# A hybrid decoder block on one core: reordering its first thirty microseconds

## The chip, the cores and the metric

The kernel runs on one core of a Trainium2 chip. The metric is the device time of one execution in microseconds; lower is better. The core has five engines that run side by side and wait for one another through semaphores: TensorE (matrix products into PSUM), VectorE, ScalarE, GpSimd and SyncE, whose queue issues most transfers.

## The reference, cut to what matters

One layer of a decoder block on x of 256 tokens by 1024 channels, in float32. What the change touches is the beginning: a normalisation, one wide projection, and the first stages of the branches.

```python
def rms_norm(x, w):
    y = xf * lax.rsqrt(jnp.mean(xf * xf, axis=-1, keepdims=True) + EPS)
    return (y * w.astype(jnp.float32)).astype(x.dtype)

def token_mixer(h, w_in, ...):
    z = h @ w_in
    rq, rk, rv, rg, sb, sc, sx, nq, nkv, ng, mg = jnp.split(z, IN_OFFSETS, axis=-1)
    y_ret = retention(...)
    y_sc = sb * causal_dwconv(sc * sx, sc_conv_w)
    k_c, v_c, k_s, v_s, k_w, v_w = jnp.split(nkv..., 6, axis=2)
    y_nsa = nsa_attention(nq, k_c, v_c, k_s, v_s, k_w, v_w, jax.nn.sigmoid(ng), ...)
    g_ret, g_sc, g_nsa = jnp.split(jax.nn.sigmoid(mg), N_BRANCH, axis=-1)
    merged = g_ret * (y_ret @ w_ret_out) + g_sc * (y_sc @ w_sc_out) + g_nsa * (y_nsa @ w_nsa_out)
    return merged @ w_mix_out

h = rms_norm(x, attn_norm_w[l])
x = x + token_mixer(h, w_in[l], ...)
h = rms_norm(x, ffn_norm_w[l])
x = x + conv_glu_ffn(h, w_ffn_up[l], ffn_conv_w[l], w_ffn_down[l])
return rms_norm(x, final_norm_w)
```

## The kernel before

**Products in three parts.** Every float32 operand is split into a rounded high half and a low half (the remainder), and a product is made as high x high + high x low + low x high (`mm3`, through `mm`, line 167). A weight comes in pieces of 1 MB, as two halves of 128 x 1024; each half is loaded by SyncE into a raw buffer (`Item.load`, L134; four buffers, `RAWB`), cast to its high half on ScalarE (L142), and the low half is subtracted on VectorE (L143). The split halves live in a ring of five pairs, and while the room `m` is idle in a sixth (`w_m`).

**The stream.** `stream` walks a list of pieces: at each it issues the loads of the pieces up to `la` ahead, splits the next one, and emits the products of the present one (`consume`) and what was put off by `later`. The program is laid out by a scheduler that may reorder instructions that do not depend on one another; `keep_in_program_order` pins one.

**The front.** x comes transposed (`xT_s`: channels on partitions, eight K-chunks of 256 tokens), chunk 0 on ScalarE's queue, the others by `head_load` (L289). `head_chunk` makes the halves `xw` of x times the norm weight, without the row scale (high on ScalarE L293, low on VectorE L294; the tiles are named ynsah and ynsal). `vv` is five items that multiply x by the value weights and the attention gates' weights (560 columns, eight K-chunks of 280 KB). They run on `xw`, and the row scale is applied to the sums (`vv_evac`, L516 and L517). Meanwhile `head_square` squares x on ScalarE (L300) and adds the squares on GpSimd (L301, L303); between the products of K-chunks 6 and 7 `head_rest` sums over the channels with four tiny products and raises to the power -1/2 on GpSimd (`row_rstd`, L307 and L308), and `head_spread` copies the result along all partitions as `rstd`. `head_h` multiplies xT_s by rstd on GpSimd (L335) and makes the scaled halves `hT` (L337 on ScalarE, L338 on VectorE).

**The order of the pieces.** Behind `vv`: kc and vc (compressed keys and values, on `xw`, scaled in `cmp_raw_evac`, L371, whose result is then moved by a transfer, dd<-dd, that ScalarE's queue issues, L372), ks and kw (keys, on `hT`), two pieces of the first merge gate (512-column products, `t_pair`, `mg_evac` L772), a w1 piece (first layer of the compression), two more gate pieces, w1, two query pieces, and so on. The first nine items run with a look-ahead of two; behind them two wide raw buffers in the rooms of x and of the squares are added, and the look-ahead is four.

Before all this stand eight warm-up products of ones (`WARM`).

Of the kernel before, what the change touches and what calls it, by code (L numbers as in the profile page):

```python
# [18 lines left out]
S = 256  # L19
# [44 lines left out]
def kernel(  # L64
# [38 lines left out]


    RAWB, SPB = 4, 5
    WARM = 8

# [14 lines left out]

    raws, loads = [raw_ring, raw_ring], [0]

    class Item:
        def __init__(self, srcs, consume, pull=0, side=0):
            self.srcs, self.consume, self.pull, self.side = srcs, consume, pull, side
            self.raw, self.parts = [], []  # L130

        def load(self):
            for (ap, n), r in zip(self.srcs, raws[loads[0] % len(raws)](len(self.srcs))):
                nc.sync.dma_start(r[:, :n], ap)  # L134
                self.raw.append(r)
            loads[0] += 1

        def split(self):
            for (ap, n), r in zip(self.srcs, self.raw):
                hi, lo = splitters[count[0] % len(splitters)](self.side)  # L140
                count[0] += 1
                A.copy(hi[:, :n], r[:, :n])  # L142
                V.tensor_sub(lo[:, :n], r[:, :n], f32(hi[:, :n]))  # L143
                self.parts.append((hi, lo))

# [144 lines left out]

    def head_chunk(k0, k1):
        for k in range(k0, k1):
            A.activation(xw[0][:, k, :], xT_s[:, k, :], AF.Copy, scale=attw(k))  # L293
            V.scalar_tensor_tensor(  # L294
                xw[1][:, k, :], xT_s[:, k, :], attw(k), f32(xw[0][:, k, :]), op0=OP.mult, op1=OP.subtract
            )

    def head_square(c):
        cs = slice(2 * c, 2 * c + 2)
        A.activation(sq[:, cs, :], xT_s[:, cs, :], AF.Square)  # L300
        G.tensor_add(sq[:, 2 * c, :], sq[:, 2 * c, :], sq[:, 2 * c + 1, :])  # L301
        if c:
            G.tensor_add(sq[:, 0, :], sq[:, 0, :], sq[:, 2 * c, :])  # L303

    def row_rstd(ps, rs):

# [22 lines left out]
    def head_spread():  # L329
        spread(rs0, sq[:, 1, :], rstd)  # L330

    def head_h(half):
        for c in range(2 * half, 2 * half + 2):
            x2k = xT_s[:, 2 * c : 2 * c + 2, :]
            G.tensor_tensor(x2k, x2k, rstd.unsqueeze(1).to_broadcast([128, 2, S]), op=OP.mult)  # L335
            for k in (2 * c, 2 * c + 1):
                A.activation(hT[0][:, k, :], xT_s[:, k, :], AF.Copy, scale=attw(k))  # L337
                V.scalar_tensor_tensor(  # L338
                    hT[1][:, k, :], xT_s[:, k, :], attw(k), f32(hT[0][:, k, :]), op0=OP.mult, op1=OP.subtract
                )  # L340
# [1 line left out]

    att_es = ExitStack()
    at = att_es.enter_context(pool("at"))
    kd = [at.tile([128, 4, 528], F32R, name=n) for n in ("kdh", "kdl")]
    vz = at.tile([128, 2, 2, 4, 128], F32R, name="vz")
    vbd = at.tile([128, 4, 4, 128], F32R, name="vbd")
    sg = at.tile([128, 2, 48], F32, name="sg")
# [12 lines left out]
    splitters.append(w_m)  # L361
    blk = {}

    def cmp_raw_evac(kv):
        def evac(ps):
            p4 = ps.rearrange("p (b t) -> p b t", b=2)
            d = cp.tile([128, 4, S], F32, tag="dd", name="dd", bufs=2)
            dv = d.rearrange("p (b two) t -> p b two t", two=2)
            for par in range(2):
                r = slice(par * 64, par * 64 + 64)  # L370
                V.tensor_tensor(dv[0:64, :, par, :], p4[r], rstd[r].unsqueeze(1).to_broadcast([64, 2, S]), op=OP.mult)  # L371
            nc.scalar.dma_start(d[64:128, :, 0 : S - 1], d[0:64, :, 1:S])  # L372
            wait_pieces(4 if kv else 2, lambda: cmp_blocks(kv, d))

        return evac

# [15 lines left out]

    def key_evac(name):
        def evac(ps):
            p4 = ps.rearrange("p (b t) -> p b t", b=2)
            kv4 = [k.rearrange("p (b two) t -> p b two t", two=2) for k in kd]
            job = []
            for par in range(2):
                r = slice(par * 64, par * 64 + 64)
                for t in range(2):  # L400
                    c = KCOL[(name, t)]
                    job.append((p4[r, :, t * 128 : (t + 1) * 128], [k[r, :, par, c : c + 128] for k in kv4]))
            for src, dst in job:
                A.copy(dst[0], src)
            for src, dst in job:
                V.tensor_sub(dst[1], src, f32(dst[0]))
            for par in range(2):
                r = slice(par * 64, par * 64 + 64)
                o = slice(64 - par * 64, 128 - par * 64)
                c = min(KCOL[(name, t)] for t in range(2))  # L410
                for k in kv4:
                    nc.gpsimd.dma_start(k[o, :, par, c : c + 256], k[r, :, par, c : c + 256])

        return evac
# [104 lines left out]
    def vv_items():  # L519
        st = {}  # L520

        def go(ks, off):
            def run(parts):
                if ks[0] == 0:
                    st["a"] = [bank("aux"), bank("aux")]
                    st["w"] = bank("aux")
                for k in ks:
                    hi, lo = parts[k - off]
                    for t in range(2):
                        a = slice(t * 128, (t + 1) * 128)  # L530
                        l = (xw[0][:, k, a], xw[1][:, k, a])
                        mm3(st["a"][t][:, 0:304], l, (hi[:, 0:304], lo[:, 0:304]), k == 0, k == 7)
                        mm3(
                            st["w"][:, t * 256 : t * 256 + 256],
                            l,
                            (hi[:, 304:560], lo[:, 304:560]),
                            k == 0 and t == 0,
                            k == 7,
                        )
                        if (k, t) == (6, 0):  # L540
                            head_rest()
                        if (k, t) == (7, 0):
                            head_spread()
                if ks[-1] == 7:
                    for t in range(2):
                        vv_evac(t, 0, st["a"][t])
                        A.activation(sg[:, t, :], st["a"][t][:, 256:304], AF.Tanh, scale=rsh[:, t : t + 1])
                        V.tensor_scalar(sg[:, t, :], sg[:, t, :], 1.0, 0.5, op0=OP.add, op1=OP.mult)  # L548
                    for t in range(2):
                        vv_evac(t, 1, st["w"][:, t * 256 : t * 256 + 256])  # L550
                    cg = sg[:, 0, :].rearrange("p (h b) -> p h b", b=3)[:, :, 0:1]
                    V.tensor_scalar(cg, cg, cmt[:, CM_ANY : CM_ANY + 1], None, op0=OP.mult)

            return run

        res = []
        for ks in ([0], [1], [2, 3], [4, 5], [6, 7]):
            res.append(Item([(wv[:, j, :], 560) for j in ks], go(ks, ks[0])))
        return res


    ynsa = []
# [203 lines left out]

    thg = {}

    def mg_evac(n, c):
        def evac(t, ps):  # L770
            th = yp.tile([128, 512], F32, tag="thg", name="thg", bufs=4)
            A.activation(th, ps, AF.Tanh, scale=0.5)  # L772
            thg[n, c, t] = th

        return evac
# [30 lines left out]
    GATE = {"o_ret": 0, "o_sc": 1, "o_nsa": 2}  # L806
    YY = {}

    def gate(n, **kw):

        return [p for c in range(2) for p in t_pair("mg", GATE[n] * 4 + 2 * c, hT, mg_evac(n, c), **kw)]

    def proj(n, **kw):
        return [p for c in range(2) for p in t_pair(n, 2 * c, lambda: YY[n], o_evac(n, c), **kw)]

    vv = vv_items()
    g_sc = gate("o_sc")
    items = vv + [
        then(piece("kc", 0, f_consume(xw, cmp_raw_evac(0), enter=True), side=SIDE), lambda: head_h(0), before=True),
        then(piece("vc", 0, f_consume(xw, cmp_raw_evac(1)), side=SIDE), lambda: head_h(1), before=True),  # L820
        piece("ks", 0, f_consume(hT, key_evac("ks")), side=SIDE),
        piece("kw", 0, f_consume(hT, key_evac("kw")), side=SIDE),
        g_sc[0],
        g_sc[1],
        piece("w1", 0, w1_consume(0, 0)),
        g_sc[2],
        g_sc[3],
        piece("w1", 1, w1_consume(0, 1)),
        nqp(0),
        nqp(1),  # L830
# [2 lines left out]
        scx(1),  # L833
        piece("w1", 3, w1_consume(1, 1)),
    ]
    vv[0].load()
    head_load(1, 2)
    vv[1].load()
    head_load(2, 4)
    vv[2].load()  # L840
    head_load(4, 6)
    head_load(6, 8)
    head_chunk(0, 1)
    vv[0].split()
    head_chunk(1, 2)
    vv[1].split()
    head_chunk(2, 4)
    vv[2].split()
    vv[3].load()
    nc.sync.dma_start(cvt, cv)  # L850
    nc.sync.dma_start(cmt, cm)
    for c in range(4):
        if c > 1:
            head_chunk(2 * c, 2 * c + 2)
        head_square(c)
    V.tensor_scalar(rethalf, x_s[:, KB : 2 * KB], 0.5, None, op0=OP.mult)
    att = attention()
    late = []
    plan = "x4 b0 x2 x3 q2 x6 b1 x5 x7 b2 q3 b3 s0 s1 n0 n1 s2 s3 n2 n3".split()
# [3 lines left out]
        late.append(made[e[0]](int(e[1])))  # L863
        late[-1].pull = (36 * (n + 1)) // len(plan) - 36 * n // len(plan)

    cut = 9
    stream(items[:cut], nxt=items[cut:])

    def wide(tag):
# [499 lines left out]
```

## Time and profile before

| | |
|---|---|
| median of 3 runs | 610.75 us (610.47 to 611.11) |
| profiled execution: its time | 611.28 us |
| profiled execution: span from first to last instruction | 609.5 us |
| TensorE busy | 597.8 us, 98% of the span |
| VectorE, ScalarE, GpSimd busy | 477.2, 388.1 and 27.0 us |
| mean granted TensorE clock | 0.998 |
| moved by transfers | 111.82 MB, mean 183 GB/s |

The busy share is an average over stages. Products are pipelined and their ends are modelled, so the starts of successive products tell more than the busy share. A row of the timeline gives start and duration of one instruction or of several merged ones (x2, x3), then engine, line, operation, output and inputs, and in brackets the idle time of the engine before it and what ended it. PE is TensorE, DVE is VectorE, ACT is ScalarE, POOL is GpSimd, SPq is SyncE's queue.

### The profile page before, as it was taken

To read this page: it belongs to the slowest core of one execution; us is meant where nothing else is said; L and a number is where in the kernel's file an instruction comes from. 1 tells how busy PE (TensorE), PEld (TensorE's weight loads), DVE (VectorE), ACT (ScalarE), POOL (GpSimd) and SP (SyncE) were. 2 spreads that over 40 slices of the span, in tenths; PEclk is the share of its full clock that TensorE was granted. 3 is DMA by queue.
4 is the path that set the end of the run, shared out by engine and by line. 5 is a ranking of instruction groups with operands and counts; after the bars stand their busy time and mean duration, and the time that the engine had idled before them with its cause. 6 is when DMAs were issued, how large, how long until landed. Compare 5 with 4: busy or idle time off the path is not lost.

```text
span 609.5 us, 10654 instructions
## 1 busy us (share of the span) xinstructions
PE 597.8 (98%) x3967; PEld 543.4 (89%) x3967; DVE 477.2 (78%) x936; ACT 388.1 (64%) x758; POOL 27.0 (4%) x36
## 2 busy tenths in 40 slices
PE   8899999999999999999999999999999999999995
PEld 7898899999999888898888888888999999999995
DVE  5788877799999878688567977568798887777754
ACT  6548865788998888644444565447756555555533
POOL 4603000000000000000000100000000000000000
PEclk9999999999999999999999999999999999999999
DMA  7789937443434444466565487575437765666401
GB/s 257 242 273 278 359 127 228 156 136 123 155 104 140 138 140 137 145 207 206 195 196 159 126 269 242 191 267 173 131 117 266 222 205 195 208 208 194 153 1 69
DMA packets 33139, 111.82 MB, mean 183 GB/s; under 512 B 3648, under 2 KB 5952, under 8 KB 32960
## 3 DMA queue, kind: packets, MB, share of 16 engines
q1 hardware_dynamic: 30384, 106.07, 53.0%
q10 hardware_dynamic: 1552, 4.03, 2.1%
q0 software_dynamic: 1152, 1.05, 1.1%
q8 instruction: 31, 0.51, 0.4%
q14 instruction: 20, 0.16, 0.1%
HBM read 108.51 MB, written 1.05 MB: 180 GB/s over the span
## 4 chain that ended last, share of the span: by engine, by line
PE 89%; ACT 3%; DVE 3%; DMA 2%; issue 1%; SPq 0%; ACTq 0%; DVEq 0%
PE ps_mm L167 66%; PE ps_aux L167 20%; PE ps_aux L642 1%; DVE wlo L143 1%; DMA xT_s<-in_xT_dram 1%; DMA raw<-in_wp_dram 1%; ACT whi L142 1%; ACT P L619 1%; PE ps_mm L797 1%; ACT ph L645 0%; DVE sg L548 0%; DVE ynsal L294 0%; PE ps_aux L671 0%; PE ps_aux L991 0%; DVE pl L646 0%
## 5 line engine op out<-in xcount | busy, mean ns | idle before, releaser
L143 DVE TENSOR_TENSOR wlo<-raw,whi 128x1024 fp32r<-128x1024 f32 (+1 forms) x187 | 225.7, 1213 | 75.1 <-ACT whi L142 73.2
L142 ACT CAST whi<-raw 128x1024 fp32r<-128x1024 f32 (+1 forms) x187 | 192.1, 1034 | 120.1 <-PE ps_mm L167 75.5
L167 PE MATMUL ps_mm<-h,whi 128*128 128x256 f32 (+1 forms) x576 | 99.0, 277 | 0.0
L167 PE MATMUL ps_mm<-hTh,whi 128*128 128x256 f32 (+1 forms) x328 | 92.2, 281 | 0.0
L167 PE MATMUL ps_mm<-hTl,whi 128*128 128x256 f32 x328 | 91.6, 279 | 0.0
L167 PE MATMUL ps_mm<-hTh,wlo 128*128 128x256 f32 x328 | 91.5, 279 | 0.0
L167 PEld LDWEIGHTS ps_mm<-h,whi 128*128 128x128 f32 x576 | 87.5, 188 | 0.7
L167 PE MATMUL ps_mm<-h,wlo 128*128 128x256 f32 x288 | 79.7, 277 | 0.0
L167 PEld LDWEIGHTS ps_mm<-hTh,whi 128*128 128x128 f32 x328 | 61.9, 189 | 0.6 <-issue 0.4
L167 PEld LDWEIGHTS ps_mm<-hTl,whi 128*128 128x128 f32 x328 | 61.8, 188 | 0.4 <-DVE hTl L338 0.2
L167 PEld LDWEIGHTS ps_mm<-hTh,wlo 128*128 128x128 f32 x328 | 61.7, 188 | 0.4
L167 PE MATMUL ps_mm<-whi,hTh 128*128 128x512 f32 x152 | 59.9, 394 | 0.0
L167 PE MATMUL ps_mm<-wlo,hTh 128*128 128x512 f32 x152 | 59.5, 392 | 0.0
L167 PE MATMUL ps_mm<-whi,hTl 128*128 128x512 f32 x152 | 59.4, 391 | 0.0
L167 PEld LDWEIGHTS ps_mm<-h,wlo 128*128 128x128 f32 x288 | 54.1, 188 | 0.0
L619 ACT ACTIVATE P<-P,st 128x16 f32<-128x16 f32 (+2 forms) x96 | 38.1, 401 | 1.1 <-DVE st L614 0.5
L167 PE MATMUL ps_aux<-wlo,acth 128*128 128x512 f32 (+1 forms) x94 | 35.5, 377 | 0.0
L167 PE MATMUL ps_aux<-whi,acth 128*128 128x512 f32 (+1 forms) x94 | 35.4, 377 | 0.0
L167 PE MATMUL ps_aux<-whi,actl 128*128 128x512 f32 (+1 forms) x94 | 35.3, 376 | 0.0
L167 PEld LDWEIGHTS ps_mm<-wlo,hTh 128*128 128x128 f32 x152 | 28.6, 188 | 6.0 <-DVE wlo L143 0.5
L167 PEld LDWEIGHTS ps_mm<-whi,hTl 128*128 128x128 f32 x152 | 28.6, 188 | 5.8
L167 PEld LDWEIGHTS ps_mm<-whi,hTh 128*128 128x128 f32 x152 | 28.6, 188 | 5.6
(263 smaller groups left out, 1200.5 us busy)
## 6 DMA issues: line engine op xcount, KB each, us to landing
raw<-in_wp_dram SPq DMA_DIRECT2D x184, 512.0 KB, 4.4
raw_w<-in_wp_dram SPq DMA_DIRECT2D x10, 512.0 KB, 6.7
raw<-in_wv_dram SPq DMA_DIRECT2D x8, 280.0 KB, 4.8
x2b<-in_xt_dram ACTq DMA_DIRECT2D x1, 1024.0 KB, 4.8
xT_s<-in_xT_dram SPq DMA_DIRECT2D x3, 256.0 KB, 6.4
rct<-in_rc_dram ACTq DMA_DIRECT2D x1, 768.0 KB, 5.0
kdh<-kdh POOLq DMA_DIRECT2D x4, 128.0 KB, 8.4
kdl<-kdl POOLq DMA_DIRECT2D x4, 128.0 KB, 9.7
```

The costliest lines, as they stand in the source:

```text
L142: A.copy(hi[:, :n], r[:, :n])
L143: V.tensor_sub(lo[:, :n], r[:, :n], f32(hi[:, :n]))
L167: return T.matmul(o, l, r, start=start, stop=stop, skip_group_check=True)
L619: A.activation(pp, pp, AF.Exp, bias=st[:, r : r + 1], scale=-1.0, accum_out=sm[:, r : r + 1])
L642: T.transpose(pt[:, dst : dst + 128], u["P"][(t, pr)][:, c : c + 128], ident)
L797: T.transpose(pt[:, b * 128 : (b + 1) * 128], src[:, c * 512 + b * 128 : c * 512 + (b + 1) * 128], ident)
```

## The change

- Loads: the loads of the value pieces, of kc and of vc are all put on SyncE's queue before any split is emitted. The last two value items load into the rooms of the key halves (`kdh`, `kdl`), vc into that of the queries (`qs`). The two constant tables (cvt, cmt) are loaded behind them.
- Order: the casts and squares of the front are pinned to one order; the first value cast is on VectorE. The row statistic stands behind the last value product, the spread of rstd behind kc's products. vc is split before the value evacuation.
- The first merge gate (four pieces) runs right behind vc, on `xw` unscaled; the row scale is applied in its tanh (`mg_evac`, `rsh`). Before each of its pieces one quarter of `hT` is made. Then w1, ks, kw, w1. The look-ahead of four begins two items later.
- Engines: the multiplication by rstd and the additions of squares go from GpSimd to VectorE; the small steps on `sg` go from VectorE to ScalarE and behind vc.
- ten warm-up products in place of eight; a 288-column first product in vc and ks.

```diff
     RAWB, SPB = 4, 5
-    WARM = 8
+    WARM = 10
 
...
 
+    exact = [False]
+
+    def in_order(ins):
+        if exact[0]:
+            tc.keep_in_program_order(ins)
+
...
             self.srcs, self.consume, self.pull, self.side = srcs, consume, pull, side
+            self.room = None
             self.raw, self.parts = [], []
...
         def load(self):
-            for (ap, n), r in zip(self.srcs, raws[loads[0] % len(raws)](len(self.srcs))):
+            room = self.room or raws[loads[0] % len(raws)]
+            for (ap, n), r in zip(self.srcs, room(len(self.srcs))):
                 nc.sync.dma_start(r[:, :n], ap)
...
 
-        def split(self):
+        def split(self, cast=A.copy):
             for (ap, n), r in zip(self.srcs, self.raw):
...
                 count[0] += 1
-                A.copy(hi[:, :n], r[:, :n])
+                in_order(cast(hi[:, :n], r[:, :n]))
                 V.tensor_sub(lo[:, :n], r[:, :n], f32(hi[:, :n]))
...
         for k in range(k0, k1):
-            A.activation(xw[0][:, k, :], xT_s[:, k, :], AF.Copy, scale=attw(k))
+            in_order(A.activation(xw[0][:, k, :], xT_s[:, k, :], AF.Copy, scale=attw(k)))
             V.scalar_tensor_tensor(
...
         cs = slice(2 * c, 2 * c + 2)
-        A.activation(sq[:, cs, :], xT_s[:, cs, :], AF.Square)
-        G.tensor_add(sq[:, 2 * c, :], sq[:, 2 * c, :], sq[:, 2 * c + 1, :])
+        in_order(A.activation(sq[:, cs, :], xT_s[:, cs, :], AF.Square))
         if c:
-            G.tensor_add(sq[:, 0, :], sq[:, 0, :], sq[:, 2 * c, :])
+            V.tensor_add(sq[:, 0:2, :], sq[:, 0:2, :], sq[:, cs, :])
+        if c == 3:
+            V.tensor_add(sq[:, 0, :], sq[:, 0, :], sq[:, 1, :])
 
...
 
-    def head_h(half):
-        for c in range(2 * half, 2 * half + 2):
+    def head_h(c):
+        if True:
             x2k = xT_s[:, 2 * c : 2 * c + 2, :]
-            G.tensor_tensor(x2k, x2k, rstd.unsqueeze(1).to_broadcast([128, 2, S]), op=OP.mult)
+            V.tensor_tensor(x2k, x2k, rstd.unsqueeze(1).to_broadcast([128, 2, S]), op=OP.mult)
             for k in (2 * c, 2 * c + 1):
...
     at = att_es.enter_context(pool("at"))
-    kd = [at.tile([128, 4, 528], F32R, name=n) for n in ("kdh", "kdl")]
+    kd = []
+
+    def key_room(tag):
+
+        z = at.tile([128, 2, 1056], F32, tag=tag, name="raw_k")
+        return lambda n: [z[:, i, 0:1024] for i in range(n)]
+
+    def query_room(n):
+        return [at.tile([128, 1024], F32, tag="qs", name="raw_q", bufs=2) for _ in range(n)]
+
...
 
-    def cmp_raw_evac(kv):
+    def cmp_raw_evac(kv, first=None):
         def evac(ps):
+            if first:
+                first()
             p4 = ps.rearrange("p (b t) -> p b t", b=2)
...
             nc.scalar.dma_start(d[64:128, :, 0 : S - 1], d[0:64, :, 1:S])
-            wait_pieces(4 if kv else 2, lambda: cmp_blocks(kv, d))
+            wait_pieces(5 if kv else 3, lambda: cmp_blocks(kv, d))
 
...
         def evac(ps):
+            if not kd:
+                kd.extend(at.tile([128, 4, 528], F32R, tag=n, name=n) for n in ("kdh", "kdl"))
             p4 = ps.rearrange("p (b t) -> p b t", b=2)
...
                         )
-                        if (k, t) == (6, 0):
-                            head_rest()
-                        if (k, t) == (7, 0):
-                            head_spread()
                 if ks[-1] == 7:
+                    head_rest()
+                    items[6].split()
                     for t in range(2):
+                        A.activation(sg[:, t, :], st["a"][t][:, 256:304], AF.Tanh, scale=rsh[:, t : t + 1])
                         vv_evac(t, 0, st["a"][t])
-                        A.activation(sg[:, t, :], st["a"][t][:, 256:304], AF.Tanh, scale=rsh[:, t : t + 1])
-                        V.tensor_scalar(sg[:, t, :], sg[:, t, :], 1.0, 0.5, op0=OP.add, op1=OP.mult)
                     for t in range(2):
                         vv_evac(t, 1, st["w"][:, t * 256 : t * 256 + 256])
-                    cg = sg[:, 0, :].rearrange("p (h b) -> p h b", b=3)[:, :, 0:1]
-                    V.tensor_scalar(cg, cg, cmt[:, CM_ANY : CM_ANY + 1], None, op0=OP.mult)
 
...
+
+    def nsa_gates():
+        for t in range(2):
+            A.activation(sg[:, t, :], sg[:, t, :], AF.Copy, scale=0.5, bias=0.5)
+        cg = sg[:, 0, :].rearrange("p (h b) -> p h b", b=3)[:, :, 0:1]
+        A.activation(cg, cg, AF.Copy, scale=cmt[:, CM_ANY : CM_ANY + 1])
 
...
 
-    def mg_evac(n, c):
+    def mg_evac(n, c, early):
         def evac(t, ps):
             th = yp.tile([128, 512], F32, tag="thg", name="thg", bufs=4)
-            A.activation(th, ps, AF.Tanh, scale=0.5)
+            A.activation(th, ps, AF.Tanh, scale=rsh[:, t : t + 1] if early else 0.5)
             thg[n, c, t] = th
...
 
-    def gate(n, **kw):
-
-        return [p for c in range(2) for p in t_pair("mg", GATE[n] * 4 + 2 * c, hT, mg_evac(n, c), **kw)]
+    def gate(n, early=False, **kw):
+
+        act = xw if early else hT
+        return [p for c in range(2) for p in t_pair("mg", GATE[n] * 4 + 2 * c, act, mg_evac(n, c, early), **kw)]
 
...
     vv = vv_items()
-    g_sc = gate("o_sc")
+    g_sc = gate("o_sc", early=True)
     items = vv + [
-        then(piece("kc", 0, f_consume(xw, cmp_raw_evac(0), enter=True), side=SIDE), lambda: head_h(0), before=True),
-        then(piece("vc", 0, f_consume(xw, cmp_raw_evac(1)), side=SIDE), lambda: head_h(1), before=True),
-        piece("ks", 0, f_consume(hT, key_evac("ks")), side=SIDE),
+        piece("kc", 0, f_consume(xw, cmp_raw_evac(0, head_spread), enter=True), side=SIDE),
+        piece("vc", 0, f_consume(xw, cmp_raw_evac(1), enter=True), side=SIDE),
+        *[then(g_sc[c], lambda c=c: head_h(c), before=True) for c in range(4)],
+        piece("w1", 0, w1_consume(0, 0)),
+        piece("ks", 0, f_consume(hT, key_evac("ks"), enter=True), side=SIDE),
         piece("kw", 0, f_consume(hT, key_evac("kw")), side=SIDE),
-        g_sc[0],
-        g_sc[1],
-        piece("w1", 0, w1_consume(0, 0)),
-        g_sc[2],
-        g_sc[3],
         piece("w1", 1, w1_consume(0, 1)),
...
     ]
+    kc, vc = items[5:7]
+    vv[3].room, vv[4].room, vc.room = key_room("kdh"), key_room("kdl"), query_room
     vv[0].load()
...
     head_load(4, 6)
+    vv[3].load()
     head_load(6, 8)
+    vv[4].load()
+    kc.load()
+    vc.load()
+    nc.sync.dma_start(cmt, cm)
+    nc.sync.dma_start(cvt, cv)
+    exact[0] = True
     head_chunk(0, 1)
-    vv[0].split()
+    vv[0].split(V.tensor_copy)
     head_chunk(1, 2)
...
     vv[2].split()
-    vv[3].load()
-    nc.sync.dma_start(cvt, cv)
-    nc.sync.dma_start(cmt, cm)
-    for c in range(4):
-        if c > 1:
-            head_chunk(2 * c, 2 * c + 2)
-        head_square(c)
-    V.tensor_scalar(rethalf, x_s[:, KB : 2 * KB], 0.5, None, op0=OP.mult)
+    head_square(0)
+    head_chunk(4, 6)
+    vv[3].split()
+    head_square(1)
+    head_chunk(6, 8)
+    vv[4].split()
+    head_square(2)
+    head_square(3)
+    exact[0] = False
+    then(vc, lambda: V.tensor_scalar(rethalf, x_s[:, KB : 2 * KB], 0.5, None, op0=OP.mult))
+    then(vc, nsa_gates)
     att = attention()
...
 
-    cut = 9
+    cut = 11
     stream(items[:cut], nxt=items[cut:])
...
```

## Rows read from the trace of the kernel before

**Rows 1.** Waits of TensorE in the first 90 us: total, times, longest

```profile
PE ps_mm L167 <- DVE wlo L143: 1.7, 1, 1.7
```

**Rows 2.** All waits of TensorE from 90 us to the end

```profile
PE ps_aux L167 <- ACT ph L645: 0.4, 2, 0.2
```

**Rows 3.** Timeline of TensorE, 0 to 36 us: start, duration, instruction

```profile
1.06 3.79 PE L167 MATMUL ps_aux<-ones 128*128 128x128 f32 x16 [1.06 <-DVE mhalf L276]
6.05 1.09 PE L167 MATMUL ps_aux<-whi,ynsah 128*128 128x304 f32 x3 [1.21 <-ACT whi L142]
...
9.07 0.60 PE L167 MATMUL ps_aux<-whi,ynsah 128*128 128x304 f32 x3
...
10.65 0.63 PE L167 MATMUL ps_aux<-whi,ynsah 128*128 128x304 f32 x3
...
16.61 0.44 PE L167 MATMUL ps_aux<-w_m,ynsah 128*128 128x304 f32 x2
...
18.13 0.30 PE L167 MATMUL ps_aux<-whi,ynsah 128*128 128x304 f32 x1
...
19.25 0.61 PE L167 MATMUL ps_aux<-ones,sq 128*128 128x1 f32 x4 [0.20 <-POOL sq L303]
19.72 0.39 PE L167 MATMUL ps_aux<-whi,ynsah 128*128 128x304 f32 x1
...
22.67 0.29 PE L167 MATMUL ps_mm<-ynsah,whi 128*128 128x288 f32 x1
...
30.63 0.39 PE L167 MATMUL ps_mm<-ynsah,wlo 128*128 128x256 f32 x1 [1.74 <-DVE wlo L143]
...
35.96 0.28 PE L167 MATMUL ps_mm<-hTh,whi 128*128 128x256 f32 x1
```

**Rows 4.** Timeline of VectorE, 10 to 26 us

```profile
10.60 1.48 DVE L143 TENSOR_TENSOR wlo<-raw,whi 128x560 fp32r<-128x560 f32 x2 [0.59 <-ACT whi L142]
...
21.35 1.22 DVE L143 TENSOR_TENSOR wlo<-raw,whi 128x1024 fp32r<-128x1024 f32 x1
22.48 0.48 DVE L517 SCALAR_TENSOR_TENSOR vz<-ps_aux,rs,vz 128x256 fp32r<-128x256 f32 x1
...
23.49 2.25 DVE L143 TENSOR_TENSOR wlo<-raw,whi 128x1024 fp32r<-128x1024 f32 x1 [0.20 <-ACT whi L142]
```

**Rows 5.** Timeline of GpSimd, 20 to 30 us

```profile
20.14 0.71 POOL L308 TENSOR_TENSOR rs<-rs,mhalf 128x2 f32<-128x2 f32 x1 [0.94 <-DMA raw<-in_wp_dram]
23.37 6.03 POOL L335 TENSOR_TENSOR xT_s<-xT_s,rstd 128x512 f32<-128x512 f32 x4 [2.52 <-DVE rstd L317]
```

**Rows 6.** Chain of waits that ended last: start, duration, what

```profile
58.93 1.89 PE ps_aux L167 x16
60.81 10.90 PE ps_mm L167 x48
```

**Rows 7.** Timeline of ScalarE, 4 to 36 us

```profile
4.94 0.51 ACT L293 ACTIVATE ynsah<-xT_s 128x256 fp32r<-128x256 f32 x1 [2.25 <-DMA xT_s<-in_xh_dram]
...
8.59 0.91 ACT L293 ACTIVATE ynsah<-xT_s 128x256 fp32r<-128x256 f32 x2 [1.06 <-DMA xT_s<-in_xT_dram]
...
9.92 1.20 ACT L142 CAST whi<-raw 128x560 fp32r<-128x560 f32 x2
...
35.81 1.05 ACT L142 CAST whi<-raw 128x1024 fp32r<-128x1024 f32 x1 [2.15 <-DVE dd L371]
```

**Rows 8.** Waits of SyncE's transfer queue, 0 to 80 us

```profile
SPq L289 <- DMA xT_s<-in_xh_dram: 0.9, 1, 0.9
```

**Rows 9.** Busy time by stretch; the last three: granted clock, transfer share, GB/s

```profile
0.00:5.00 5.00, 3.79 (x16) 3.49 (x16) 0.23 (x3) 1.54 (x3) 2.44 (x7) 1.00 0.62 176
5.00:10.00 5.00, 3.95 (x19) 3.93 (x20) 3.40 (x7) 3.94 (x9) 0.74 (x1) 1.00 0.93 308
10.00:15.00 5.00, 4.79 (x34) 4.22 (x32) 4.40 (x8) 4.90 (x12) 3.20 (x4) 1.00 0.87 299
...
30.00:35.00 5.00, 4.37 (x38) 4.38 (x39) 4.97 (x9) 3.66 (x7) 0.00 (x0) 1.00 0.51 166
```

## The prediction

> **What bounds the kernel now.** I read the waits of TensorE first. In the first 90 us it waits for VectorE's low weight halves and for little else [rows 1]; in the remaining 519.5 us one wait stands, of 0.4 us in all [rows 2]. So this is a TensorE-bound kernel: its end is set by when TensorE falls into continuous work, plus work that the change leaves as it is. What can be won lies between the first real product and that point.
>
> The timeline of TensorE shows how much that is [rows 3]. The warm-up products run from 1.06 to 4.85, then comes 1.21 us of nothing; the first value product starts at 6.05. Its first K-chunk (12 products, of 304 and 256 columns) takes until 9.07, 3.02 us; the next takes until 10.65, 1.58 us, and a later one (16.61 to 18.13) 1.52 us. [...] Value products and row statistic end at 22.67, kc runs from there with a hole of 1.74 us before 30.63, and the first product on hTh (piece ks) starts at 35.96.
>
> Where the hole comes from is seen on VectorE and GpSimd. kc's first low half took VectorE 1.22 us, the second 2.25 us, in just the time in which GpSimd scales xT_s by rstd (23.37 to 29.40) [rows 4, 5]. The chain of waits then turns to TensorE alone, and its rows give the price of the later pieces: two gate pieces (48 products of 512 columns) 10.90 us, a w1 piece 1.89 us [rows 6].
>
> **The change part by part, priced against the profiled execution** (span 609.5 us, time 611.28 us, 0.53 us above the median of 610.75).
>
> *First product.* Today ScalarE makes x's first high half (4.94 to 5.45) and then vv0's [rows 7]. The change moves vv0's to VectorE. No row shows this cast there: two ScalarE casts of this size take 1.20 us [rows 7], two VectorE subtractions 1.48 us [rows 4], so it is 0.6 to 0.74 us from 4.94 at the latest. The first product comes at 5.55 to 5.75; I take 5.6, 0.45 us earlier.
>
> *Clock.* Two more warm-ups fill 0.47 us each (3.79 us for eight), so they end near 5.8 if placed as before and the gap closes. With the first chunk still at the lower level, chunk 0 ends at 5.6 + 3.02 = 8.6 and chunk 1 at 10.2; at the higher level, at 8.7. Either way chunk 2 waits for data, as follows, so I count nothing. [...]
>
> *Value chunks 2 to 7.* x chunks 2 and 3 are turned from 8.59 on, when they land, until 9.50 [rows 7]. The pinned order puts vv2's casts right behind (0.6 each: 10.1, 10.7), and VectorE's first subtraction ends at about 10.85. Chunk 2 then ends at about 11.85 (today it starts at 10.65 and waits inside). ScalarE goes on without a hole: square 0.52, x4 and x5 0.85, vv3 1.15 (13.2), square 0.52, x6 and x7 0.85, vv4 1.15 (15.7); VectorE follows each by some 0.75, and vv3's first low half is there at 13.4, when TensorE comes to it. From chunk 3 on TensorE is the limit: 11.85 + 5 x 1.52 = 19.45. Transfers allow it: the stretches of five microseconds moved 0.88, 1.54 and 1.50 MB [rows 9]; all of x and the values is 3.4 MB, there by 13.3, kc by 17 and vc by 20. They are not really issued at once: already today an xT load waited 0.9 us for xh to land, a ninth load while eight are under way [rows 8], and the new pieces will queue in the same way. That costs nothing, because the engines have work ahead.
>
> *Square sums and row statistic.* Three additions of 512 columns and one of 256 go from GpSimd to VectorE. No row has them there; nearest are a 256-column pass, 0.48, and the 560-column subtraction, 0.74 [rows 4]; I take 0.7 for 512 columns and 0.4 for 256, 2.5 us in all (1.9 to 3.0 at the bounds). They are done at about 18.5, before 19.45. The statistic takes TensorE 0.47 us (19.25 to 19.72 today) [rows 3]: 19.9.
>
> *kc and vc.* 22.67 to 35.96 is 13.29 us; less the 1.74 hole and 0.2 of slow restart it is 11.35 us of products. kc's halves are ready (ScalarE 15.7, squares 1.1, kc 2.0: 18.8; VectorE 18.5 + 2 x 1.22 = 20.9, needed when half of kc is through, at 22.7), vc's at 23.3, needed at 25.6. The hole is gone because nothing on GpSimd reads SBUF beside them. The spread of rstd now stands between kc and vc, 0.47 us of TensorE (as the statistic). Sum: 19.9 + 11.35 + 0.47 = 31.7, against 35.96: **4.25 us earlier**.
>
> *Gates ahead of ks and kw, unscaled.* The same 96 products; they read xw, so the multiplication by rstd has 21 us to run under them. On VectorE it is 4 x 0.74 = 3.0 us (GpSimd needed 6.03). sg's small steps go to ScalarE after vc. VectorE's whole list from 18.5 to the first w1 piece (kc, vc, four gate pieces and w1: 14 x 1.22; scale 3.0; hT low halves 8 x 0.48; for evacuations, vz and blocks I estimate 8 from the same rows) is 31.9 us, done at 50.4; TensorE needs it at 31.7 + 21.8 = 53.5. Nothing is added or lost here.
>
> *No cost:* the borrowed kd and qs rooms (first written again tens of microseconds later), cvt and cmt behind vc (first used after 25), rethalf, two 288-column starts. If the cover of the cmt load were gone, it would delay only sg, which attention reads far behind.
>
> So the span of 609.5 becomes 605.25, and the median 610.75 - 4.25 = **606.5 us**. The later work has no wait that could swallow the shift [rows 2].
>
> **The rivals.**
>
> 1. *The row scale is late behind VectorE.* Statistic, pow on GpSimd, spread and copy are a chain, and VectorE now has kc's and vc's subtractions (4 x 1.22) in front of its short steps; what is queued behind on ScalarE is the dd transfer's issue, which already once kept ScalarE idle for 2.15 us [rows 7]. If the spread's operand comes after all of vc's halves and the vz evacuations, TensorE stands 1 to 3.7 us between kc and vc (3.7 is three subtractions): 608.5 with 2. [...] Against the rival: by the list above the spread has from 19.9 to 25.6. Chance 0.13.
>
> 2. *VectorE falls behind between w1 and nq.* ks, kw and w1 come together, with key evacuations and vc's blocks between, and VectorE has taken 5.5 us of GpSimd's work. Slack there is 1 to 3 us. A late piece or two costs 1 to 3 us: 608.5 with 2. Against: the contention, 1.03 us on one subtraction alone, is gone. Chance 0.14.
>
> 3. *More is won:* chunk 2's data are there at 9.0 instead of 10.85 and the clock's level lets TensorE use it: 604.7. Needs the loads to land earlier than the 8.59 that the trace shows. Chance 0.08.
>
> 4. *Slower: transfers starve the gates.* The wide prefetch room opens two pieces later, so the gates live on four raw buffers. At the worst rate seen while ScalarE waited for loads, 166 GB/s [rows 9], a piece of 1.05 MB takes 6.3 us against TensorE's 5.45. Three gate pieces lose 0.85 each, the w1 piece of 1.89 loses 4.4, ks another 0.8: 7.8 us, 614.3 less what is loaded ahead by then, one piece or two: 612.5. It decides from 4.25 us lost, that is below some 190 GB/s. Against: 299 and 308 GB/s when the queue is full. Chance 0.07.
>
> 5. *The shift is given back:* the hole moves to another place in equal size, say to the start of the gates, where the dd issue holds ScalarE: 610 to 611. Chance 0.06.
>
> **How the numbers follow.** My forecast has 0.52, with a range of its own from 605.3 to 607.7 (first product and additions at their bounds, plus or minus half a microsecond of later order). Faster by over 0.2% (1.2 us, about what a measurement of this kernel can tell) is the forecast and rivals 1 to 3, less a little for their tails: 0.84; within 0.2% rival 5 and tails, 0.08; slower 0.08. Leaving out rival 4, half of 5 and the outer tails, the range is 604.2 to 609.4.
>
> **What would show it.** After the change: first value product near 5.6; values and statistic through at 19.9; the first gate product near 31.7 and no wait of over 0.3 us between; VectorE's 1024-column subtractions at 1.22 everywhere; first ks product near 55; no new wait of TensorE around w1. Wrong would be: TensorE waiting for the spread or for whi/wlo at kc, vc or the first gate, or ScalarE idle for landings between 30 and 55 with TensorE behind it.

## The result and the profile after

The changed kernel takes 606.17 us (median of 4 runs, 605.71 to 606.73) against 610.61 for the kernel before, measured beside it: a ratio of 0.9928, 95% interval 0.9916 to 0.9939, 4.4 us less. The forecast was 606.5. The profiled execution took 606.51 us, with a span of 604.7 us against 609.5.

TensorE's waits in the first 90 us after the change (total, times, longest):

```profile
PE ps_aux L175 <- DVE mhalf L284: 1.1, 1, 1.1
PE ps_aux L175 <- DVE whi L150: 1.0, 1, 1.0
PE ps_aux L175 <- DVE wlo L151: 0.4, 1, 0.4
PE ps_aux L175 <- ACT whi L150: 0.3, 1, 0.3
```

No wait on ps_mm is left; the one of 1.7 us [rows 1] is gone. The timeline of TensorE at the places that were priced:

```profile
1.06 4.50 PE L175 MATMUL ps_aux<-ones 128*128 128x128 f32 x20 [1.06 <-DVE mhalf L284]
6.54 0.63 PE L175 MATMUL ps_aux<-whi,ynsah 128*128 128x304 f32 x3 [0.98 <-DVE whi L150]
...
10.49 0.40 PE L175 MATMUL ps_aux<-whi,ynsah 128*128 128x304 f32 x1 [0.33 <-ACT whi L150]
11.27 0.41 PE L175 MATMUL ps_aux<-wlo,ynsah 128*128 128x304 f32 x1 [0.37 <-DVE wlo L151]
...
20.38 0.50 PE L175 MATMUL ps_aux<-ones,sq 128*128 128x1 f32 x4
20.74 0.38 PE L175 MATMUL ps_mm<-ynsah,whi 128*128 128x288 f32 x1
...
32.26 0.40 PE L175 MATMUL ps_mm<-whi,ynsah 128*128 128x512 f32 x1
...
55.93 0.30 PE L175 MATMUL ps_mm<-hTh,whi 128*128 128x288 f32 x1
```

kc begins 1.93 us earlier than in [rows 3], and the piece behind vc (now a gate piece) at 32.26 in place of 35.96, 3.70 us earlier. The span shrank by 4.8, so 1.1 us more is won behind that point. The chain that ended last shows where: from 11.27 it is TensorE alone (start, duration, what).

```profile
11.27 9.61 PE ps_aux L175 x75
20.88 5.59 PE ps_mm L175 x48
26.47 0.48 PE ps_aux L175 x4
26.95 27.25 PE ps_mm L175 x144
54.21 1.89 PE ps_aux L175 x16
56.09 10.92 PE ps_mm L175 x96
```

The last row is ks and kw: 96 products in 10.92 us. Before, the same 96 took from 35.96 to 47.52, 11.56 us. There hT's last low halves were still being made (37.29 to 38.96 on VectorE), and a weight load of TensorE waited 0.2 us for one; that this is the whole of the 0.64 us is not shown. Another 0.3 us lies in the first two gate pieces (11.24 us before, 10.9 after), where before a weight load waited 0.5 us for a low half.

Nothing is won up to the third chunk (chunk 2). Chunk 3 begins where it began before, while the prediction ends chunk 2 at 11.85 (first row before, second after):

```profile
12.74 0.30 PE L167 MATMUL ps_aux<-whi,ynsah 128*128 128x304 f32 x1
12.77 0.31 PE L175 MATMUL ps_aux<-whi,ynsah 128*128 128x304 f32 x1
```

On VectorE the two halves of kc now take the same time, and the row scale stands under gate products:

```profile
18.43 1.22 DVE L151 TENSOR_TENSOR wlo<-raw,whi 128x1024 fp32r<-128x1024 f32 x1
19.57 0.42 DVE L312 TENSOR_TENSOR sq<-sq 128x256 f32<-128x256 f32 x1
19.90 1.22 DVE L151 TENSOR_TENSOR wlo<-raw,whi 128x1024 fp32r<-128x1024 f32 x1
...
27.52 0.42 DVE L326 COPY rstd<-ps_aux 128x256 f32<-128x256 f32 x1
...
32.68 0.69 DVE L344 TENSOR_TENSOR xT_s<-xT_s,rstd 128x512 f32<-128x512 f32 x1
```

The prediction, and the texts below that follow it, put the hole of 1.74 us at kc. The rows place it one piece later: kc's 48 products run from 22.67 to 28.49 without it, and TensorE then stands for vc's first low half, which before stood on VectorE behind kc's slowed second half and slowed small steps on sg:

```profile
25.67 1.27 DVE L548 TENSOR_SCALAR sg<-sg 128x48 f32<-128x48 f32 x1
...
28.10 1.34 DVE L548 TENSOR_SCALAR sg<-sg 128x48 f32<-128x48 f32 x1
29.36 1.21 DVE L143 TENSOR_TENSOR wlo<-raw,whi 128x1024 fp32r<-128x1024 f32 x1
```

So far the main steps fit the prediction. But it puts the whole gain down to kc and vc coming forward, and counts the new order of the gates as nothing. The experiments test that.

### The profile page after: what moved, and what is told of

Read it like the earlier page. It is cut to its first block, busy times and chain, and to the rows that moved or that the text cites. A ratio compares the mean times of both kernels' runs of the same rounds, so it can differ in the third digit from the quotient of the medians.

```text
span 604.7 us, 10654 instructions
## 1 busy us (share of the span) xinstructions
PE 594.8 (98%) x3971; PEld 541.7 (90%) x3971; DVE 476.4 (79%) x942; ACT 387.8 (64%) x760; POOL 14.7 (2%) x25
## 4 chain that ended last, share of the span: by engine, by line
PE 92%; ACT 3%; DVE 3%; DMA 1%; issue 1%; SPq 0%; POOL 0%; ACTq 0%; POOLq 0%
PE ps_mm L175 68%; PE ps_aux L175 21%; PE ps_aux L665 1%; DMA xT_s<-in_xT_dram 1%; DVE wlo L151 1%; ACT whi L150 1%; ACT P L642 1%; ACT ph L668 0%; PE ps_aux L694 0%; DVE hnb L1097 0%; PE ps_mm L820 0%; PE ps_aux L1024 0%; DVE x2b L1096 0%; DVE pl L669 0%; ACT hnb L1246 0%
## 5 line engine op out<-in xcount | busy, mean ns | idle before, releaser
L151 DVE TENSOR_TENSOR wlo<-raw,whi 128x1024 fp32r<-128x1024 f32 (+1 forms) x185 | 223.3, 1211 | 72.4 <-ACT whi L150 70.3
L175 PE MATMUL ps_mm<-hTh,whi 128*128 128x256 f32 (+1 forms) x320 | 89.9, 281 | 0.0
L175 PE MATMUL ps_mm<-hTh,wlo 128*128 128x256 f32 x320 | 89.1, 278 | 0.0
L175 PE MATMUL ps_mm<-hTl,whi 128*128 128x256 f32 x320 | 89.0, 278 | 0.0
L175 PE MATMUL ps_mm<-whi,hTh 128*128 128x512 f32 x128 | 50.5, 395 | 0.0
L175 PE MATMUL ps_mm<-wlo,hTh 128*128 128x512 f32 x128 | 50.0, 391 | 0.0
L175 PE MATMUL ps_mm<-whi,hTl 128*128 128x512 f32 x128 | 50.0, 391 | 0.0
L749 ACT ACTIVATE uu<-ps_mm,cvt 128x256 f32<-128x256 f32 x36 | 16.9, 469 | 22.5 <-DVE uu L751 16.1
L175 PEld LDWEIGHTS ps_mm<-whi,hTl 128*128 128x128 f32 x128 | 24.1, 188 | 4.9
L175 PEld LDWEIGHTS ps_mm<-whi,hTh 128*128 128x128 f32 x128 | 24.0, 188 | 4.8
```

The source lines that it names most:

```text
L175: return T.matmul(o, l, r, start=start, stop=stop, skip_group_check=True)
L749: A.activation(o, z, AF.Copy, scale=w[2])
```

## The experiments

Names beginning with a are the changed kernel with an edit, with b the kernel before with an edit, with c an attempt at a better one. The kernel before ran beside them on the same chips, at medians of 610.54 to 610.69. "Theory A" is mine at the time; it changed once, after the first four.

**First four: warm-up, order, the scale's engine.**

```diff
 a_warm8
-    WARM = 10
+    WARM = 8
```

> The changed kernel with 8 warm-up products in place of 10. [...] Rival: the earlier rise of the clock is part of the gain, and the time is 1.0 to 1.5 us longer, 607.2 to 607.7.

606.22 us (606.03 to 606.46). By stretch (TensorE's products in the first bracket, granted clock third from the end):

```profile
6.00:9.95 3.95, 3.89 (x16) 3.92 (x17) 3.55 (x7) 2.85 (x6) 0.00 (x0) 1.00 1.00 367
9.95:15.00 5.05, 5.05 (x42) 5.05 (x41) 4.82 (x10) 5.05 (x12) 0.00 (x0) 1.00 1.04 411
```

Here 16 products take 3.95 us and then 42 take 5.05. Products of 256 columns begin 0.21 to 0.22 us apart up to 9.96 and 0.12 us apart from there, and the record of the granted clock begins at 9.95, with 1.00 (the 1.00 of the first row has no record behind it). The slower pace, which a_late_gate below has at a granted clock of 0.50, is what is called the lower level here. With ten warm-ups the changed kernel's record begins at 5.30, its first products of 256 columns begin 0.12 us apart, and its first chunk (12 products) takes 1.94 us. The time is the same. Theory A, the prediction's, that chunk 2 waits for its data whatever the pace of chunks 0 and 1, holds: TensorE has slack until those data are there.

```diff
 a_late_gate
-g_sc = gate("o_sc", early=True)
+g_sc = gate("o_sc")
-        *[then(g_sc[c], lambda c=c: head_h(c), before=True) for c in range(4)],
-        w1, ks, kw, w1, ...
+        then(ks, lambda: [head_h(c) for c in range(4)], before=True),
+        kw, g_sc[0], g_sc[1], w1, g_sc[2], g_sc[3], w1, ...
-    cut = 11
+    cut = 9
```

(`wait_pieces` is also put back to 4 and 2.)

> The changed kernel with the first merge gate back behind ks and kw, on the scaled halves, and all four quarters of hT made before ks; all else of the change stays. Theory A (the gate pieces give the row scale its cover): ks needs hT at 32.3, rstd is there at 27.9, and behind it stand 2.8 us of scale, 3.5 us of low halves and the splits of ks on VectorE, so TensorE waits 2 to 4 us at ks and the time is 608 to 610. Rival (the early gate is only another order of the same products): less than 0.5 us, 606.2 to 606.7.

610.57 us (609.82 to 611.66), ratio 1.0001, interval 0.9992 to 1.0011: the gain is gone to the last tenth, though kc still begins at 19.64. By stretch:

```profile
31.20:33.89 2.69, 0.71 (x5) 0.39 (x3) 2.61 (x5) 1.05 (x3) 0.00 (x0) 1.00 0.90 253
33.89:37.30 3.41, 3.21 (x12) 2.70 (x13) 3.41 (x6) 1.85 (x4) 0.00 (x0) 0.50 1.02 252
```

and in the waits:

```profile
PE ps_mm L175 <- ACT hTh L346: 2.1, 2, 1.9
```

TensorE stands for 1.9 us for hT; then its granted clock is 0.50 for 3.4 us (products of 256 columns begin 0.21 us apart; 0.11 at 41, where it is 1.00 again), with VectorE full (3.41 of 3.41 us). The chain that ended last runs through VectorE in that time, at its end through ScalarE, and comes to TensorE only when the granted clock is about to return to 1.00 (at 37.30):

```profile
34.60 1.82 DVE xT_s L344 x3
36.41 0.50 ACT hTh L346
...
36.96 20.99 PE ps_mm L175 x131
```

So VectorE's list (splits, scale, dd, halves of hT) holds TensorE up until 36.96, and the low level costs next to nothing here. The other executions bear this out: 3.4 us at 0.50 take the mean clock of 608.6 us down to 0.997 at best, eight of the ten have a mean of 0.998 or 0.999, and the median of those eight is 610.6 too. Theory A was right in kind and 0.6 us short of the size.

```diff
 a_pool_scale, b_dve_scale (the same line, each way)
-            V.tensor_tensor(x2k, x2k, rstd..., op=OP.mult)
+            G.tensor_tensor(x2k, x2k, rstd..., op=OP.mult)
```

> The changed kernel with the multiplication by rstd on GpSimd again. Theory A (GpSimd's reads slow VectorE's subtractions, and that is what delayed kc): subtractions beside the scale take 2.2 in place of 1.22 us again, but now under 21 us of gate products, so TensorE waits little: 606.2 to 607.0. Rival (moving the scale to VectorE is itself what removes the hole): the hole of 1 to 2 us comes back at the first gate piece, 607.2 to 608.2.

605.83 us (605.28 to 606.15), no worse than the changed kernel. VectorE and GpSimd:

```profile
29.31 4.39 DVE L151 TENSOR_TENSOR wlo<-raw,whi 128x1024 fp32r<-128x1024 f32 x2
...
26.98 7.87 POOL L344 TENSOR_TENSOR xT_s<-xT_s,rstd 128x512 f32<-128x512 f32 x4 [6.08 <-DVE rstd L326]
```

Two subtractions take 4.39 us beside GpSimd, as in [rows 4, 5], and TensorE doesn't notice. Theory A holds. The hole does not come back either, though GpSimd has the scale again: it starts at 26.98, behind vc's last subtraction (23.13 to 24.35). So in the changed kernel it is the place of the scale that keeps the hole away, and the engine adds nothing.

> The kernel before, with one edit: the multiplication by rstd on VectorE in place of GpSimd. Theory A (contention made the hole of 1.74 us at kc): kc's second low half takes 1.22 us, the small steps on sg 0.2 us, the hole shrinks by 1.5 us or more and the time is 608.9 to 609.5. Rival (VectorE is full there, so 2.8 us of more work takes the place of the slowing): the hole stays or moves to ks, 610.3 to 611.5.

611.73 us (609.90 to 614.65), ratio 1.0021, 1.0005 to 1.0038: not faster. Stretches kc with vc, then ks with kw:

```profile
22.45:33.76 11.31, 11.31 (x98) 11.31 (x97) 9.21 (x19) 8.31 (x15) 0.00 (x0) 1.00 0.85 270
33.76:48.58 14.82, 11.92 (x99) 11.32 (x97) 14.60 (x22) 8.56 (x15) 2.50 (x4) 1.00 0.80 237
```

The hole is gone (11.31 us for kc and vc in place of 13.29), and the small steps on sg are short:

```profile
24.32 0.18 DVE L548 TENSOR_SCALAR sg<-sg 128x48 f32<-128x48 f32 x1
```

So GpSimd's scale did cause the hole. But ks and kw now take 14.82 us in place of 11.56, with VectorE busy for 14.60 of them: the scale and the halves of hT queue behind the splits. A late load has a part in it that this run does not separate: ScalarE makes hT's high halves behind a cast that waited 3.00 us for its load, and VectorE stood 1.98 us for them.

```profile
30.46 1.05 ACT L142 CAST whi<-raw 128x1024 fp32r<-128x1024 f32 x1 [3.00 <-DMA raw<-in_wp_dram]
...
31.95 1.68 DVE L338 SCALAR_TENSOR_TENSOR hTl<-xT_s,hTh 128x256 fp32r<-128x256 f32 x4 [1.98 <-ACT hTh L337]
```

Of the two theories the first had the cause right, the rival the time.

**Next four: order alone, rooms, sums, first casts.** Theory A from here on: kc forward and the early gate each pay only with the other.

b_gate_order puts the early gate, on `xw` with `rsh` in the tanh, and then w1, ks, kw into the kernel before; `wait_pieces` as after; loads, engines and row statistic stay.

> The kernel before, with the order alone: the first merge gate right behind vc on the unscaled halves, w1, then ks and kw; loads, engines and row statistic as before (the row scale still on GpSimd and beside kc). Theory A (the order gives cover to hT, the other parts bring kc forward, and each gains only with the other): the hole of 1.7 us at kc stays, about 1 us of waits at ks goes, 609.3 to 610.0. Rival (the order is the whole change): 606.5 to 607.5.

611.87 us (610.41 to 613.49), ratio 1.0021, 1.0008 to 1.0033. Both too low. The hole at vc shrinks to 0.56 us, but a wait of 1.04 us for a low half stands at the first gate piece. Waits of TensorE, and ScalarE where the last one arises:

```profile
PE ps_mm L167 <- DVE wlo L143: 1.6, 2, 1.0
...
PE ps_mm L167 <- ACT thg L772: 0.9, 1, 0.9
```

```profile
48.15 1.05 ACT L142 CAST whi<-raw 128x1024 fp32r<-128x1024 f32 x1 [4.54 <-DMA raw<-in_wp_dram]
49.10 0.68 ACT L772 ACTIVATE thg<-ps_mm,rsh 128x512 f32<-128x512 f32 x1
```

A gate's tanh, which frees a bank of `ps_mm`, stands in ScalarE's queue behind a cast that waited 4.54 us for its load; TensorE waits for the bank. This is rival 4's place (transfers late under the gates), and a wait that I had not listed.

```diff
 a_raw_ring
-    vv[3].room, vv[4].room, vc.room = key_room("kdh"), key_room("kdl"), query_room
-    vv[3].load()
     head_load(6, 8)
+    vv[3].load()
     vv[4].load()
```

> The changed kernel without the borrowed rooms: the last two value items and vc load into the four raw buffers and wait for them as in the kernel before (the last x chunks are put ahead of them). Theory A (early loads give only the second half of kc in time): kc's second half lands near 22, its low half is ready near 24.5 against a need at 23.6, and vc follows: 0.5 to 1.5 us longer, 606.7 to 607.7. Rival (the early loads are what brings kc forward by 2 to 3 us): 608.5 or more.

608.22 us (607.62 to 609.50), 2.1 us longer than the changed kernel, between the two. Its waits have the same bank wait, and a late sum:

```profile
PE ps_mm L175 <- ACT thg L795: 0.9, 1, 0.9
...
PE ps_aux L175 <- DVE sq L312: 0.8, 1, 0.8
```

So the borrowed rooms pay in two places: ahead of the row statistic, and 27 us later in the lead of the loads under the gates. The edit also puts the last x chunks ahead of the values; what that alone is worth was not tested.

```diff
 a_pool_sums
-            V.tensor_add(sq[:, 0:2, :], sq[:, 0:2, :], sq[:, cs, :])   (and the last of 256 columns)
+        G.tensor_add(sq[:, 2 * c, :], sq[:, 2 * c, :], sq[:, 2 * c + 1, :])
+            G.tensor_add(sq[:, 0, :], sq[:, 0, :], sq[:, 2 * c, :])
```

> The changed kernel with the additions of squares on GpSimd as before. Theory A (hidden in front of the row statistic, which now stands behind all value products): 606.0 to 606.7. Rival (GpSimd's reads slow the subtractions of the value halves, which TensorE follows closely): value products end 1 us later or more, 607.2 or more.

609.09 us (607.61 to 609.52), 2.9 us longer than the changed kernel: the rival's time, by another mechanism. GpSimd, and then stretches of the core:

```profile
18.25 1.72 POOL L309 TENSOR_TENSOR sq<-sq 128x256 f32<-128x256 f32 x1
20.04 1.59 POOL L311 TENSOR_TENSOR sq<-sq 128x256 f32<-128x256 f32 x1
```

```profile
17.00:22.30 5.30, 3.73 (x30) 3.53 (x29) 4.05 (x3) 2.49 (x3) 4.47 (x4) 1.00 1.02 389
22.30:25.72 3.42, 3.42 (x17) 3.42 (x18) 2.57 (x7) 2.41 (x7) 0.71 (x1) 0.50 0.68 243
```

The last sum takes 1.59 us beside kc's subtractions and ends at 21.63; TensorE waits 1.6 us for it, and in this execution its granted clock is 0.50 for 3.4 us afterwards. Here the low level does cost: kc's 48 products take 7.30 us on the chain that ended last, in place of 5.59. The two of the seven executions with a mean clock of 0.998, too high for such a stretch, take 607.61 and 607.92, 1.4 and 1.8 us above the changed kernel, about the wait alone; the five with 0.994 to 0.996 take 608.45 to 609.52. VectorE's work on the value halves is slowed too (two low halves of x in 1.71 us, 0.88 in the changed kernel), but TensorE does not wait longer for them; it waits for the statistic behind them.

```diff
 c_front
-    head_chunk(0, 1)
     vv[0].split(V.tensor_copy)
+    head_chunk(0, 1)
     ...
-    vv[2].split()
+    vv[2].split(first=V.tensor_copy)
```

> The changed kernel with two casts placed otherwise: vv0's cast on VectorE ahead of x's first chunk in the pinned order, and the first half of vv2 cast on VectorE too. Theory A (the waits of TensorE left in the first 12 us are set by these casts): first product at 5.5 in place of 6.0 to 6.5, chunk 2's low half 0.3 us earlier, 0.3 to 0.6 us shorter, 605.6 to 605.9. Rival (landings set both): within 0.2 us of 606.2.

605.79 us (605.64 to 606.07). The first product comes at 5.54, but TensorE then waits for the low halves (0.69 and 0.37 us) and kc begins at 20.60.

**Last four: the scatter of the small differences, and the late gate once more.**

> The changed kernel itself, beside the next two on the same chip. 605.8 to 606.4 by both theories.

605.86 us (604.61 to 606.39): the median of the changed kernel itself moves by 0.3 us from one run to another, so a_pool_scale and c_front are not told from it. From one execution to another the front moves more: in this run's profile x landed at 8.04 and kc began at 19.81, against 8.96 and 20.74 above.

> The changed kernel with the earlier first casts on VectorE and the row scale back on GpSimd. Theory A (the row scale's engine is of no account under the gate products, and the first casts give some tenths): 605.3 to 605.9, below the changed kernel by 0.3 to 0.6 us. Rival (the two small gains of before were scatter): within 0.2 us of the changed kernel.

606.05 us (605.73 to 606.55). The rival holds: no gain.

a_act_cast takes `V.tensor_copy` out of vv0's split.

> The changed kernel with vv0's cast on ScalarE again. Theory A (chunk 2 waits for its data whatever the first product does): first product at about 6.0, end as in the changed kernel within 0.3 us. Rival (the cast on VectorE is what makes the front quick): 0.4 us or more longer.

605.94 us (605.58 to 606.21): no difference, though the first product comes at 5.54, earlier than expected. VectorE's cast buys nothing.

a_late_gate_pool is a_late_gate with `G.tensor_tensor` for the row scale.

> The changed kernel with the late gate (ks and kw right behind vc, as in the run a_late_gate) and the row scale on GpSimd. [...] Rival (the chain from the row statistic alone makes hT late): 609.8 to 611.

612.99 us (612.14 to 614.64), ratio 1.0045: above the rival's range, and above the 607 to 609 of Theory A, by which the scale on a free GpSimd starts at once and brings hT in time. Its wait, VectorE, and stretches:

```profile
PE ps_mm L175 <- DVE hTl L347: 4.1, 2, 3.5
```

```profile
28.97 4.37 DVE L151 TENSOR_TENSOR wlo<-raw,whi 128x1024 fp32r<-128x1024 f32 x2
33.27 1.48 DVE L347 SCALAR_TENSOR_TENSOR hTl<-xT_s,hTh 128x256 fp32r<-128x256 f32 x1
```

```profile
31.00:35.13 4.13, 0.59 (x5) 0.37 (x4) 4.10 (x4) 1.91 (x5) 3.47 (x2) 1.00 0.97 243
35.13:41.95 6.82, 6.28 (x30) 5.99 (x29) 6.16 (x11) 2.46 (x4) 0.00 (x0) 0.50 1.00 281
```

The scale does start at once, and hT's high half is early, but the low half waits behind two subtractions slowed to 4.37 us (2.36 in a_late_gate). TensorE stands 3.5 us and then runs 6.8 us at a granted clock of 0.50 (30 products in 6.28 us busy, then 68 in 8.05 at 1.00), with one more wait of 0.5 us. The chain that ended last comes to it here:

```profile
36.74 23.87 PE ps_mm L175 x136
```

That is 17.4 us behind kc's first product (19.32); in a_late_gate it was 17.3 us behind (36.96 after 19.64). So up to there the two late gates are level, and the 2.4 us between them lie behind it, where this run is at 0.50 for another 5.2 us; by the two paces that costs an estimated 2.3 us. All five executions have a mean clock of 0.992 to 0.995, those of a_late_gate 0.996 to 0.999. So the scale's engine matters by 2.4 us under the late gate, through the granted clock, and not measurably under the early one.

## Why the prediction was right

The sum, step by step, against the profiled execution:

- *First product* 5.6 forecast, 6.54 measured. VectorE took x's first low half ahead of the cast, which ran from 5.95. a_act_cast and c_front show that this costs nothing.
- *Clock* "I count nothing": shown by a_warm8. With two more warm-ups the record of the granted clock, at 1.00, begins at 5.30, while they ran, against 9.95, and the time did not move. The gap did not close (0.98 us are left before the first product).
- *Chunk 2* first low half at 10.85 forecast; the product that uses it started at 11.27 (x landed at 8.96, not 8.56). The sum then let 1.0 us remain of chunk 2; only one of its 12 products had run by then, and the others took 1.50 us, to 12.77.
- *Values and statistic* 19.9 forecast, 20.74 measured: 0.4 from the late half of chunk 2, 0.5 from the rest of that chunk, less 0.1 at the statistic (0.36 us).
- *kc, spread, vc* 11.82 forecast, 11.52 measured. That GpSimd's scale caused the hole (at vc, not at kc) is shown by b_dve_scale: with the scale on VectorE kc's second low half took 1.22 us in place of 2.25, and the hole was gone. With it back on GpSimd in a_pool_scale, two subtractions took 4.39 us, against 2.36 in the changed kernel.
- *Gates forward* 31.7 forecast, 32.26 measured; 96 products in 21.8 us as priced.
- *"Nothing is added or lost here"*, of the gates ahead of ks and kw, is the step that was mis-sized. 1.1 us was won behind that point, and what the order holds up is far more: without it the time is 610.57. The reason for the zero (21 us of cover for the scale) was right; what it costs if that cover is gone, 4.4 us, was not priced.
- *Square sums* were priced as VectorE's work only. Left on GpSimd they cost 2.9 us, as a wait and as slow products.

That the number came so close is partly luck. In the profiled executions the gates came 0.56 us later than forecast and 1.1 us was won behind them that the sum does not have; the two misses partly cancel. Most of the gain, 3.7 of 4.8 us, came before the gates as forecast, but the picture of one added gain at kc was wrong. The parts don't add: b_dve_scale is 1.2 us above the kernel before by medians, b_gate_order 1.2 above, the changed kernel without the order is level with it, without the sums 1.6 below, without the rooms 2.5 below, and the whole 4.4 below. Bringing kc forward only moves the wait to ks unless the gates stand between; the gates alone wait for VectorE's low halves (1.6 us) and, behind a late load, for a bank (0.9 us).

The rivals: the scale's chain (1) did not fall behind: the spread's products began 26.31, right after kc's last. pow took 0.71 us from 21.27, with VectorE idle for it (0.83 us), so what it takes beside a subtraction was not put to the test. VectorE (2) had no shortfall around w1. The 166 GB/s that price rival 4 were read where ScalarE waited for dd (2.15 us, [rows 7]) and not for a load. Rival 4's mechanism was seen in b_gate_order and a_raw_ring at 0.9 us, and not in the changed kernel, where ScalarE also idled for a load under the gates, up to 4.75 us, but the bank was free in time. What stays open: how long TensorE waits in the other executions of a_late_gate, of which only one was profiled, and what the pinned order and the new places of the row statistic and the spread are worth, which no run undid.

## What to carry to other kernels

Where a normalisation's scale can be applied to a product's sum, the pieces that allow it belong between the row statistic and the first piece that needs the scaled operand: they are the cover for the scale. Before moving work to another engine, ask whether its consumer is covered: under the gates the engine made no difference, without them it made 2.4 us, in slow products behind a longer wait. And take changes of one front apart by undoing each, not by doing each alone: here two parts done alone were each a loss.

## What was not expected of the hardware

A wait of TensorE of 1.6 to 1.9 us was followed by 3.4 us at a granted clock of 0.50 in two kernels, and one of 3.5 us by 6.8 us; the kernel before has a hole of 1.74 us [rows 3] after which the granted clock stayed at 1.00 [rows 9]. So a hole of that length can be followed by the low level or not, and the executions of a_pool_sums and a_late_gate differ in this among themselves, by their mean clocks. What the level costs depends on who is late: 1.7 us at kc in a_pool_sums, where TensorE was the limit, and next to nothing in a_late_gate, where VectorE was. What decides whether the granted clock falls was not tested.
